# Moving two attention buffers by 128 bytes and several operands further into their places, in a one-core FoX/MLA decoder kernel

## The chip, the cores and the metric

The kernel runs on one core of one Trainium2 chip. The metric is device time in microseconds (us) of one launch. The kernel before takes 1050.32 us (median of 3 runs, 1049.77 to 1051.04). One further run was recorded by the hardware profiler; all rows of the profile come from that one.

## The reference, cut to what matters

One sequence of 256 tokens of width 1024 passes through two layers, in float32. A layer is a half feed-forward step, a mixer, a second half feed-forward step and a gated per-layer embedding, each followed by a layer norm. The mixer is a "forgetting" attention (FoX, 16 heads of 64) in layer 0 and a multi-head latent attention (MLA, 16 heads) in layer 1:

```python
x = post_norm(x, 0.5 * swiglu(x, w_in, w_out), ...)      # D_FF = 2816
x = post_norm(x, fox_mixer(...) if layer == 0 else mla_mixer(...), ...)
x = post_norm(x, 0.5 * swiglu(x, w_in2, w_out2), ...)
x = post_norm(x, sigmoid(x @ Wg + bg) * (p[i] @ Wp), ...)

def mla_mixer(x, w_dq, q_norm, w_uq, w_o, k_nope, k_rope, v, cos, sin):
    c_q = rms_norm(x @ w_dq, q_norm)                       # 384 latents per token
    q = jnp.einsum('bsc,chd->bshd', c_q, w_uq)             # 16 heads x (128 + 64)
    s = q_nope . k_nope + rope(q_rope) . k_rope            # causal, blocks of 128 queries
    o = softmax(s * 192 ** -0.5) . v
    return o.reshape(B, S, 16 * 128) @ w_o
```

The keys and values of the MLA layer come from 256 latents per token and one rotated key of 64 that all heads share (`shared_kv`).

## The kernel before, in words

**Numbers in two halves.** TensorE multiplies in the fp32r type. To keep float32 accuracy each operand is held as a rounded half ("hi") and a rest ("lo"), and each product is three matmuls that add into one PSUM bank: hi by hi, hi by lo, lo by hi (`mm3`, whose matmuls are all recorded under L616). A weight arrives by DMA as a 1 MB group in a raw buffer (`raw`); ScalarE writes hi (L252, L260), VectorE subtracts and writes lo (L253, L264). The pair goes to one of ten slots, which the profile calls `hl`. Activations are split in the same way out of PSUM: `high` (L629, ScalarE) and then `low` (L633, VectorE), which reads hi and so runs behind it.

**Two operands of a matmul.** One operand is loaded into the array and stays (a PEld row); the other streams past it (the PE row). The loading of the next one overlaps the streaming of the present one. Which of the two a weight is depends on the step: in the bulk of the first feed-forward product the weights (`wiu`) are loaded and the transposed stream `xT` moves; in its first columns (`win`) and in many other products (`fv`, `kvv`, `qr`, `pg`, `wout`, `fo`, `mo`) the weights move past a loaded activation.

**Where a buffer lies.** Pools place the tiles one behind another in each partition of on-chip memory, so that a tile's size sets the byte positions of all behind it. `place` (L221) puts a split weight into its slot of 2112 words; `moves` (L427) named the weights that start 48 words (192 bytes) into it: `fv` and `pg 0`. The rest start at word 0. Four buffers, `fs`, `qk`, `ota` and `otb` ("homes"), hold the hidden activations in the feed-forward steps and something else in the mixers. In the MLA layer `qk` holds the queries and keys of two heads, `ota` and `otb` the transposed attention outputs, `gb` the transposed query latents (`cqt`), and a part of `fs` the rotated keys (`kr`). With the sizes of before the slots, `fs`, `qk`, `gb` and `P` begin at 224 modulo 256 bytes, `xT` at 160, and `ota` and `otb` at 96.

**The order of work in the MLA layer.** A list written out by hand, `ORDER` (L71), names 527 steps; each emits its instructions at once, so the list sets the order on every engine. The steps of one head h: `gen` computes query and key in a PSUM bank, `ga` and `gd` write them into `qk` (ScalarE hi, VectorE lo), `QK` multiplies them (six matmuls of `tr<-qk` and three of `tr<-fs,xT`, which is the rotated part), `mi` adds the mask and takes minima (VectorE, L1717 and L1720), `ex` is the exponential (ScalarE, L1730), `T`, `ta` and `td` transpose the weights of attention into `PT`, `AV` multiplies with the values, `oa` and `od` write the result to `ota` or `otb`, and `O h` multiplies it with the output weights (`y<-hl,otb` and `y<-hl,ota`). Steps `f`, `l` and `a` split further weights meanwhile. `qk` holds heads of even and odd number apart: the index `s = h % 2` in `gen` and `h % 2` in `QK`. The list runs ahead: head h+1's `gen`, `ga` and `gd` often stand before `QK h`, for instance

```python
"f 1", "gen 6", "ga 6", "T 4", "ta 4", "td 4", "gd 6",
"tr 4", "a", "QK 5", "a", "a", "a", "mi 5", ...
```

**What sets the waits.** No wait is written by hand. The framework notes which part of which tile an instruction reads or writes, and where two instructions of different engines touch the same part it puts a semaphore wait on the later one. How finely parts are told apart follows from the shape in which the tile was made and how it is sliced.

Of the kernel before, what the change touches and what calls it, by code (L numbers as in the profile page):

```python
# [11 lines left out]
F32R = mybir.dt.float32r  # L12
# [132 lines left out]
class Stream:  # L145
# [74 lines left out]

    def place(self, key, slot):  # L221
        w = self.pool.tile([128, 2112], F32R, tag=slot, name=slot, bufs=1)
        c = 48 if moves(key) else 0
        return w[:, c : c + 2048].rearrange("p (i c) -> p i c", i=2)

    def split(self, half=False):
        self.later()
        nc = self.nc
        key = self.order[self.ready]
        g = group_of(key)  # L230
        while self.sums_left(key):
            self.add(g)
        src, parts, n = unit_of(key, self.raw[g], self.sums.get(g))
        if self.aside(key):
            w = self.pool.tile([128, 2, 512], F32R, tag="g4", name="g4", bufs=6)
        else:
            slot = self.slots.pop(0)
            self.slot_of[key] = slot
            w = self.place(key, slot)
        hi, lo = w[:parts, 0, :n], w[:parts, 1, :n]  # L240
        shape = src.shape
        if len(shape) == 3:
            hi = hi.rearrange("p (a b) -> p a b", b=shape[2])
            lo = lo.rearrange("p (a b) -> p a b", b=shape[2])
        elif len(shape) == 4:
            hi = hi.rearrange("p (a b c) -> p a b c", b=shape[2], c=shape[3])
            lo = lo.rearrange("p (a b c) -> p a b c", b=shape[2], c=shape[3])
        t = self.arrives[group_of(key)]
        self.act_t, self.dve_t = max(self.act_t, t), max(self.dve_t, t)

        def both():
            nc.scalar.activation(hi, src, AF.Copy)  # L252
            nc.vector.tensor_tensor(lo, src, hi.bitcast(F32), op=ALU.subtract)  # L253

        if key[0] == "pb":
            nc.gpsimd.memset(w[:, 0, :].bitcast(F32), 0.0)
            lo = w[32:33, 0, :n]
            both()
        elif half:
            nc.scalar.activation(hi, src, AF.Copy)  # L260
            self.busy(act=n)

            def rest():
                nc.vector.tensor_tensor(lo, src, hi.bitcast(F32), op=ALU.subtract)  # L264
                self.busy(dve=n)
                self.split_done(key, w)

            self.rest = rest
            return
        else:  # L270
            both()
        self.pair(n)
        self.split_done(key, w)

    def aside(self, key):
# [148 lines left out]
    return key  # L424


def moves(key):  # L427
    return key[0] == "fv" or key[:2] == ("pg", 0)


def unit_of(key, raw, sums=None):

    k, u = key[0], key[-1] % 2
    if k in ("win", "fv"):
        return raw.rearrange("p (k c) -> p k c", c=512)[:, 2 * u : 2 * u + 2, :], 128, 1024
    if k == "wiu":
        return raw[:, 1024 * u : 1024 * u + 1024], 128, 1024
    if k == "ws":
        i = key[-1]
        return ((raw, sums)[i // 2])[:, 1024 * u : 1024 * u + (512 if i == 3 else 1024)], 128, 512 if i == 3 else 1024  # L440
    if k == "fvc":
        n = 816 if key[-1] < 2 else 544
        return raw[:, n * u : n * u + n], 128, n
    if k in ("wout", "fvb", "fo", "pg", "pp", "mo", "qr"):
        return raw[:, 1024 * u : 1024 * u + 1024], 128, 1024
    if k in ("fk", "fq"):
        return raw.rearrange("p (k c) -> p k c", c=256)[:, :, 128 * u : 128 * u + 128], 128, 1024
    if k == "pb":
        return raw[0:1, 0:1024], 1, 1024
    if k == "kd":  # L450
        return raw[:, 640 * u : 640 * u + 640], 128, 640
    if k == "dq":
        return raw[:, 768 * u : 768 * u + 768], 128, 768
    if k == "qn":
        return raw[:, 512:1280], 128, 768
    if k == "kvv":
        return raw[:, 0:1024], 128, 1024
    if k == "kvk":
        return raw[:, 0:512], 128, 512
    raise KeyError(key)  # L460
# [50 lines left out]
class Trunk:  # L511
# [612 lines left out]
    def fox(self, li):  # L1124
        nc, S, a = self.nc, self.S, self.a
# [26 lines left out]
        def VC(t, at={}):  # L1152

            ps = self.bank("y")
            for k in range(8):
                if k in at:
                    at[k]()
                if k % 3 == 0:
                    w = self.use(("fvc", k // 3))
                c = 272 * (k % 3)  # L1160
                self.mm3(
                    ps[:, 0:272], lambda i: self.xT[:, t, i, k, :], lambda i: w[:, i, c : c + 272], k == 0, k == 7)
            if (t, 1) not in v:
# [1 line left out]
            o = v[t, 1]  # L1165
# [28 lines left out]
        f, e, u, r, ab = (fs[fr, 256 * i : 256 * i + 256] for i in range(5))  # L1194
# [79 lines left out]
        qk = self.own([128, 2, 2, 512], F32R, "qk")  # L1274
# [200 lines left out]

    def kv_transpose_rope(self):
        nc = self.nc
        self.kr = self.kvt[:, 1088:1856].rearrange("p (i t c) -> p t i c", t=2, i=3)
        kr = [self.kr[:, :, i, :] for i in range(3)]
        b = self.bank("tr")  # L1480
        for t in range(2):
# [20 lines left out]
    def mla(self, li):  # L1502
# [3 lines left out]
            self.dma(qn, pbcast(a["mla_q_norm"][0], QR))  # L1506
        scale = float(192 ** -0.5)
        v = {}
        cqt = self.tl([128, 2, 2, 3, 128], F32R, "gb", 1)
        cqtok = self.tl([128, 2, 768], F32, "PT", 1)  # L1510
        S.reclaim("otb", "qk")
        home = {}
# [163 lines left out]

        def gen(h):
            if h == 0:
                o = self.own([128, 2, 1072], F32R, "qk")
                home["qk"] = o[:, :, 0:1024].rearrange("p w (t i s c) -> p w t i s c", t=2, i=2, s=2)  # L1680
            ps = self.bank("h")
            hp, s = h // 2, h % 2
# [252 lines left out]
```

## Time and profile before

| | |
|---|---|
| median of 3 runs | 1050.32 us (1049.77 to 1051.04) |
| time of the profiled execution | 1049.6 us |
| its span (first to last instruction) | 1047.8 us |
| TensorE matmul (PE) | 1035.6 us busy, 99% of the span, 7085 matmuls |
| TensorE weight load (PEld) | 948.6 us, 91%, beside PE |
| VectorE (DVE) | 891.8 us, 85% |
| ScalarE (ACT) | 592.9 us, 57% |
| GpSimd (POOL) | 58.0 us, 6% |
| data moved | 202.74 MB, mean 193 GB/s |
| mean granted TensorE clock | 0.998 |

The profiled execution's own time is 1.8 us above its span, which is what lies around the first and the last instruction. A row of the timeline gives the start and the length in us of a run of like instructions, the engine, the line, the operation, `out<-in` by the program's buffer names, the shape, and how many it joins. In the length of a row of joined matmuls the pipelined end of the last is contained, so that the time of one matmul is better read as the start of the next row less the start of this one, over the count.

### The profile page before, as it was taken

How to read it: one execution, taken by the hardware profiler on the slowest of the kernel's cores; microseconds unless marked ns; L12 is line 12 of the kernel's file. 1: busy time of each engine (PE TensorE's matmuls, PEld its weight loads, DVE VectorE, ACT ScalarE, POOL GpSimd, SP SyncE). 2: the span in 40 equal slices, each digit the busy share in tenths (PEclk: the TensorE clock that was granted, in tenths of full speed). 3: DMA queues.
4: the chain of work that ended last, by engine and by line, in shares of the span. 5: the costliest groups of instructions: out<-in, count | busy, mean ns of one | idle time of the engine just before them, and what ended most of it. 6: DMA issues, size and time to landing. Idle time of an engine off the chain costs nothing.

```text
span 1047.8 us, 17555 instructions
## 1 busy us (share of the span) xinstructions
PE 1035.6 (99%) x7085; PEld 948.6 (91%) x7085; DVE 891.8 (85%) x1312; ACT 592.9 (57%) x901; POOL 58.0 (6%) x88
## 2 busy tenths in 40 slices
PE   9999999999999999999999999999999999999996
PEld 8999898899889999998899898988999889898986
DVE  5788977868898979978979899888887989889877
ACT  6555563666755555663565646646776564646541
POOL 0000000122300000000220000000000000000000
PEclk9999999999999999999999999999999999999999
DMA  7855586455636363673674545743445564555732
GB/s 281 305 191 188 185 298 243 162 168 169 216 128 246 121 252 125 241 282 132 236 260 151 195 169 190 270 142 112 145 156 179 183 214 162 200 190 176 271 125 81
DMA packets 37476, 202.74 MB, mean 193 GB/s; under 512 B 3970, under 2 KB 9874, under 8 KB 16532
## 3 DMA queue, kind: packets, MB, share of 16 engines
q1 hardware_dynamic: 37396, 201.63, 54.3%
q8 instruction: 55, 0.90, 0.3%
q14 instruction: 25, 0.20, 0.1%
HBM read 200.55 MB, written 1.06 MB: 192 GB/s over the span
## 4 chain that ended last, share of the span: by engine, by line
PE 95%; DVE 2%; ACT 1%; issue 1%; DMA 0%; SPq 0%; DVEq 0%; ACTq 0%
PE h L616 53%; PE y L616 29%; PE tr L616 10%; PE tr L620 2%; DVE hl L253 1%; PE h L620 1%; DMA raw<-in_w_dram 0%; PE tr L1375 0%; DVE ts L300 0%; DVE x L705 0%; DVE tr L1720 0%; ACT qk L629 0%; DVE PT L633 0%; DVE ts L306 0%; DVE raw L308 0%
## 5 line engine op out<-in xcount | busy, mean ns | idle before, releaser
L616 PE MATMUL h<-xT,hl 128*128 128x256 f32 x3144 | 366.1, 277 | 1.2 <-ACT hl L327 0.7
L616 PEld LDWEIGHTS h<-xT,hl 128*128 128x128 f32 x3144 | 362.0, 188 | 2.9 <-ACT hl L327 1.2
L253 DVE TENSOR_TENSOR hl<-raw,hl 128x1024 fp32r<-128x1024 f32 (+5 forms) x271 | 314.2, 1190 | 36.1 <-ACT hl L252 35.0
L252 ACT ACTIVATE hl<-raw 128x1024 fp32r<-128x1024 f32 (+5 forms) x271 | 267.8, 1027 | 70.6 <-DVE raw L308 41.3
L616 PE MATMUL y<-hl,g 128*128 128x512 f32 x336 | 78.6, 391 | 0.0
L616 PEld LDWEIGHTS y<-hl,g 128*128 128x128 f32 x336 | 62.5, 188 | 12.6
L616 PE MATMUL h<-hl,xT 128*128 128x512 f32 (+2 forms) x312 | 67.9, 371 | 0.0
L616 PEld LDWEIGHTS h<-hl,xT 128*128 128x128 f32 x312 | 54.9, 188 | 9.8
L616 PE MATMUL y<-hl,otb 128*128 128x512 f32 x219 | 58.0, 399 | 0.0
L264 DVE TENSOR_TENSOR hl<-raw,hl 128x1024 fp32r<-128x1024 f32 (+2 forms) x44 | 52.3, 1192 | 0.8 <-ACT hl L260 0.7
L616 PE MATMUL y<-hl,xT 128*128 128x512 f32 (+3 forms) x282 | 52.7, 334 | 0.0
L260 ACT ACTIVATE hl<-raw 128x1024 fp32r<-128x1024 f32 (+2 forms) x44 | 45.2, 1029 | 9.7 <-DVE raw L308 9.1
L629 ACT ACTIVATE xT<-tr 128x512 fp32r<-128x512 f32 x28 | 16.1, 597 | 58.9 <-PE tr L620 58.9
L616 PEld LDWEIGHTS y<-hl,xT 128*128 128x128 f32 x282 | 44.1, 188 | 4.6 <-ACT xT L629 0.4
L616 PEld LDWEIGHTS y<-hl,otb 128*128 128x128 f32 x219 | 39.8, 188 | 8.4 <-DVE otb L633 0.3
L616 PE MATMUL y<-hl,ota 128*128 128x512 f32 x177 | 46.8, 398 | 0.1
L700 POOL TENSOR_TENSOR rs<-ve,mhalf 128x1 f32<-128x1 f32 x16 | 15.1, 942 | 519.8 <-DVE ve L699 519.8
L616 PE MATMUL tr<-xT,hl 128*128 128x256 f32 x360 | 42.5, 277 | 0.0
L616 PEld LDWEIGHTS tr<-xT,hl 128*128 128x128 f32 x360 | 41.7, 188 | 0.4
L616 PEld LDWEIGHTS y<-hl,ota 128*128 128x128 f32 x177 | 32.7, 189 | 7.7 <-DVE hl L253 0.6
L823 ACT ACTIVATE P<-h 128x512 f32<-128x512 f32 x33 | 19.7, 596 | 33.0 <-PE h L616 32.6
L300 DVE TENSOR_TENSOR ts<-raw 128x1024 f32<-128x1024 f32 x29 | 35.4, 1222 | 0.6
(322 smaller groups left out, 1632.7 us busy)
## 6 DMA issues: line engine op xcount, KB each, us to landing
raw<-in_ffn_in_dram SPq DMA_DIRECT2D x85, 1024.0 KB, 5.0
raw<-in_ffn_out_dram SPq DMA_DIRECT2D x44, 1024.0 KB, 5.0
raw<-in_pg_dram SPq DMA_DIRECT2D x8, 1024.0 KB, 4.9
raw<-in_mo_dram SPq DMA_DIRECT2D x8, 1024.0 KB, 4.8
raw<-in_kq_dram SPq DMA_DIRECT2D x8, 640.0 KB, 4.2
gb<-in_ln_g_dram SPq DMA_DIRECT2D x8, 512.0 KB, 5.9
gb<-in_ln_b_dram SPq DMA_DIRECT2D x8, 512.0 KB, 7.5
raw<-in_fk_dram SPq DMA_DIRECT2D x4, 1024.0 KB, 5.6
```

Of the source, the lines that this page charges most:

```text
L252: nc.scalar.activation(hi, src, AF.Copy)
L253: nc.vector.tensor_tensor(lo, src, hi.bitcast(F32), op=ALU.subtract)
L260: nc.scalar.activation(hi, src, AF.Copy)
L264: nc.vector.tensor_tensor(lo, src, hi.bitcast(F32), op=ALU.subtract)
L300: tt(s[:, 0:1024].rearrange("p (a b) -> p a b", b=512), r[:, 0:512][:, None, :].to_broadcast([128, 2, 512]), r[:, 512:1536].rearrange("p ( ...
L616: self.nc.tensor.matmul(out, lhsT, rhs, start=start, stop=stop)
L620: self.nc.tensor.transpose(out, in_, self.ident)
L629: self.nc.scalar.activation(hi, src, AF.Copy)
L700: nc.gpsimd.tensor_tensor(rs, ve, self.mhalf, op=ALU.pow)
L823: nc.scalar.activation(gt, ps, AF.Silu)
```

## The change

Two kinds of edits. The first is in `place` and in the sizes of tiles. A table `shift` takes the place of `moves`: the weights `win` (but for the first feed-forward step of layer 0), `kvv` and `qr` start 48 words into their slots too, as `fv` and `pg 0` did; `fvb` and `fvc` start 32 words in, `kd` 36 and `dq` 40. The three column blocks of `fvc` lie 320 words apart in place of 272. The rotated keys start at word 1120 of their buffer in place of 1088 (128 bytes), and the query latents 48 words into `gb`. The second is in `gen`: the `qk` tile is made as one flat row of 2176 words, whose first 2144 are then viewed as two parts of 1072, where it was made as [128, 2, 1072]. It is 32 words (128 bytes) longer, so that `ota` and `otb`, and what lies behind them, lie 128 bytes further on. `ota` and `otb` then begin at 224 modulo 256.

```diff
--- before.py
+++ after.py
@@ -220,7 +220,7 @@
 
     def place(self, key, slot):
         w = self.pool.tile([128, 2112], F32R, tag=slot, name=slot, bufs=1)
-        c = 48 if moves(key) else 0
+        c = shift(key)
         return w[:, c : c + 2048].rearrange("p (i c) -> p i c", i=2)
 
     def split(self, half=False):
@@ -240,8 +240,9 @@
         hi, lo = w[:parts, 0, :n], w[:parts, 1, :n]
         shape = src.shape
         if len(shape) == 3:
-            hi = hi.rearrange("p (a b) -> p a b", b=shape[2])
-            lo = lo.rearrange("p (a b) -> p a b", b=shape[2])
+            b = n // shape[1]
+            hi = hi.rearrange("p (a b) -> p a b", b=b)[:, :, 0 : shape[2]]
+            lo = lo.rearrange("p (a b) -> p a b", b=b)[:, :, 0 : shape[2]]
         elif len(shape) == 4:
             hi = hi.rearrange("p (a b c) -> p a b c", b=shape[2], c=shape[3])
             lo = lo.rearrange("p (a b c) -> p a b c", b=shape[2], c=shape[3])
@@ -269,7 +270,7 @@
             return
         else:
             both()
-        self.pair(n)
+        self.pair(math.prod(shape[1:]))
         self.split_done(key, w)
 
     def aside(self, key):
@@ -424,8 +425,11 @@
     return key
 
 
-def moves(key):
-    return key[0] == "fv" or key[:2] == ("pg", 0)
+def shift(key):
+
+    if key[0] in ("fv", "kvv", "qr") or key[:2] == ("pg", 0) or key[0] == "win" and key[1:3] != (0, "ffn1"):
+        return 48
+    return {"fvb": 32, "fvc": 32, "kd": 36, "dq": 40}.get(key[0], 0)
 
 
 def unit_of(key, raw, sums=None):
@@ -440,7 +444,7 @@
         return ((raw, sums)[i // 2])[:, 1024 * u : 1024 * u + (512 if i == 3 else 1024)], 128, 512 if i == 3 else 1024
     if k == "fvc":
         n = 816 if key[-1] < 2 else 544
-        return raw[:, n * u : n * u + n], 128, n
+        return raw[:, n * u : n * u + n].rearrange("p (a b) -> p a b", b=272), 128, n // 272 * 320
     if k in ("wout", "fvb", "fo", "pg", "pp", "mo", "qr"):
         return raw[:, 1024 * u : 1024 * u + 1024], 128, 1024
     if k in ("fk", "fq"):
@@ -1157,7 +1161,7 @@
                     at[k]()
                 if k % 3 == 0:
                     w = self.use(("fvc", k // 3))
-                c = 272 * (k % 3)
+                c = 320 * (k % 3)
                 self.mm3(
                     ps[:, 0:272], lambda i: self.xT[:, t, i, k, :], lambda i: w[:, i, c : c + 272], k == 0, k == 7)
             if (t, 1) not in v:
@@ -1475,7 +1479,7 @@
 
     def kv_transpose_rope(self):
         nc = self.nc
-        self.kr = self.kvt[:, 1088:1856].rearrange("p (i t c) -> p t i c", t=2, i=3)
+        self.kr = self.kvt[:, 1120:1888].rearrange("p (i t c) -> p t i c", t=2, i=3)
         kr = [self.kr[:, :, i, :] for i in range(3)]
         b = self.bank("tr")
         for t in range(2):
@@ -1506,7 +1510,7 @@
             self.dma(qn, pbcast(a["mla_q_norm"][0], QR))
         scale = float(192 ** -0.5)
         v = {}
-        cqt = self.tl([128, 2, 2, 3, 128], F32R, "gb", 1)
+        cqt = self.tl([128, 1584], F32R, "gb", 1)[:, 48:1584].rearrange("p (t i k c) -> p t i k c", t=2, i=2, k=3)
         cqtok = self.tl([128, 2, 768], F32, "PT", 1)
         S.reclaim("otb", "qk")
         home = {}
@@ -1676,7 +1680,7 @@
 
         def gen(h):
             if h == 0:
-                o = self.own([128, 2, 1072], F32R, "qk")
+                o = self.own([128, 2176], F32R, "qk")[:, 0:2144].rearrange("p (w c) -> p w c", w=2)
                 home["qk"] = o[:, :, 0:1024].rearrange("p w (t i s c) -> p w t i s c", t=2, i=2, s=2)
             ps = self.bank("h")
             hp, s = h // 2, h % 2
```

No instruction is added, removed or reordered on any engine, as far as the names go. The waits differ. The lines of the changed kernel's matmuls are numbered L620 (L616 before) and its transposes L624 (L620 before).

First place: TensorE around `QK 2` in the MLA layer. The rows `tr_7712<-qk` are that step, `tr_7704<-ident,P` the transpose before it, `h_7747<-PT` the attention output after it. Before:

```order
L616 MATMUL h_7697<-p_7667,g_7358 128x128 [waits Activation_49]
L620 MATMUL tr_7704<-ident,P 128x128 x3
L616 MATMUL tr_7712<-qk 128x256 [waits PE_49]
L616 MATMUL tr_7712<-qk 128x128
L616 MATMUL tr_7712<-fs,xT 128x256
L616 MATMUL tr_7712<-qk 128x256 x3
L616 MATMUL tr_7712<-fs,xT 128x256 x2
L616 MATMUL h_7747<-PT,g_7383 128x256 [waits DVE_49,Activation_49]
L616 MATMUL h_7747<-PT,g_7383 128x256 [waits DVE_49]
```

and in the changed kernel:

```order
L620 MATMUL h_7697<-p_7667,g_7358 128x128 [waits Activation_49]
L624 MATMUL tr_7704<-ident,P 128x128 x3
L620 MATMUL tr_7712<-qk 128x256 [waits DVE_49]
L620 MATMUL tr_7712<-qk 128x128
L620 MATMUL tr_7712<-fs,xT 128x256
L620 MATMUL tr_7712<-qk 128x256 x3
L620 MATMUL tr_7712<-fs,xT 128x256 x2
L620 MATMUL h_7747<-PT,g_7383 128x256 [waits Activation_49]
L620 MATMUL h_7747<-PT,g_7383 128x256 [waits DVE_49]
```

The first matmul of `QK 2` waited on a TensorE count and now waits on a VectorE count, and the first matmul behind the step has lost its VectorE wait.

Second place: TensorE around `QK 5`, where `h_7923` (rows with `fs,hl` and `gb,hl`) is `gen 6`, `tr_7953<-qk` is `QK 5`, and `y_7732<-hl_7788,otb` is the output product that follows. Before:

```order
L616 MATMUL h_7923<-gb,hl_7846 128x256 x9
L620 MATMUL tr_7940<-ident,P 128x128 [waits PE_49,Activation_49]
L620 MATMUL tr_7940<-ident,P 128x128 [waits Activation_49]
L620 MATMUL tr_7940<-ident,P 128x128
L616 MATMUL tr_7953<-qk 128x256 [waits DVE_49]
L616 MATMUL tr_7953<-qk 128x128
L616 MATMUL tr_7953<-fs,xT 128x256
L616 MATMUL tr_7953<-qk 128x256 x3
L616 MATMUL tr_7953<-fs,xT 128x256 x2
L616 MATMUL y_7732<-hl_7788,otb 128x512 [waits Activation_49]
L616 MATMUL y_7732<-hl_7788,otb 128x512
L616 MATMUL y_7732<-hl_7788,otb 128x512 [waits DVE_49]
```

and in the changed kernel:

```order
L620 MATMUL h_7923<-gb,hl_7846 128x256 x9
L624 MATMUL tr_7940<-ident,P 128x128 [waits PE_49,Activation_49]
L624 MATMUL tr_7940<-ident,P 128x128 [waits Activation_49]
L624 MATMUL tr_7940<-ident,P 128x128
L620 MATMUL tr_7953<-qk 128x256 [waits DVE_49,Activation_49]
L620 MATMUL tr_7953<-qk 128x128
L620 MATMUL tr_7953<-fs,xT 128x256
L620 MATMUL tr_7953<-qk 128x256 x3
L620 MATMUL tr_7953<-fs,xT 128x256 x2
L620 MATMUL y_7732<-hl_7788,otb 128x512 x3
L620 MATMUL y_7733<-hl_7788,otb 128x512 x3
```

The first matmul of `QK 5` waited on VectorE alone and now waits on VectorE and ScalarE. The ScalarE and the VectorE wait of the output product behind it are gone, since `QK 5` has waited for more by then.

Third place: VectorE at `gd 11`, the write of lo of head 11 (`qk<-h_8347`), which stands behind `QK 10` in the list. `otb<-h_8329` is the attention output's lo, `tr_8372` the scores of `QK 10`. Before:

```order
L633 TENSOR_TENSOR otb<-h_8329,otb 128x256 [waits Activation_49]
L253 TENSOR_TENSOR hl_8342<-raw,hl_8342 128x768 [waits Activation_49]
L633 TENSOR_TENSOR qk<-h_8347,qk 128x2x2x128 [waits Activation_49]
L633 TENSOR_TENSOR PT<-tr_8364,PT 128x2x128 [waits PE_49,Activation_49]
L1717 TENSOR_TENSOR P<-tr_8372,mask 128x128 [waits PE_49]
L1720 ISA tr_8372,nm<-tr_8372,P 128x128 [waits DVE_49]
```

and in the changed kernel:

```order
L637 TENSOR_TENSOR otb<-h_8329,otb 128x256 [waits Activation_49]
L254 TENSOR_TENSOR hl_8342<-raw,hl_8342 128x768 [waits Activation_49]
L637 TENSOR_TENSOR qk<-h_8347,qk 128x2x2x128 [waits PE_49]
L637 TENSOR_TENSOR PT<-tr_8364,PT 128x2x128 [waits Activation_49]
L1721 TENSOR_TENSOR P<-tr_8372,mask 128x128 [waits PE_49]
L1724 ISA tr_8372,nm<-tr_8372,P 128x128 [waits DVE_49]
```

The write waited on ScalarE alone, and now on TensorE.

## The prediction

> **What bounds the kernel now.** I read the page's first lines, the chain of waits, and the stretch with the MLA attention from the busy times by stretch.
>
> ```profile
> span 1047.8 us, 17555 instructions
> PE 1035.6 (99%) x7085; PEld 948.6 (91%) x7085; DVE 891.8 (85%) x1312; ACT 592.9 (57%) x901; POOL 58.0 (6%) x88
> PE 95%; DVE 2%; ACT 1%; issue 1%; DMA 0%; SPq 0%; DVEq 0%; ACTq 0%
> 730.00:810.00 80.00, 79.47 (x544) 72.53 (x543) 67.82 (x169) 57.48 (x145) 0.00 (x0) 1.00 0.44 149
> ```
>
> TensorE matmul sets the time: 95% of the chain, and in the stretch from 730 to 810 us it is busy for 79.47 of 80, with VectorE at 67.82 and ScalarE at 57.48. So two things move the end: how fast matmuls follow each other, and any wait that stops TensorE. The change touches both.
>
> **Part 1, the places: matmuls follow each other faster.** Matmuls of one shape don't all take the same time here. In one feed-forward product of layer 0 the stationary operand comes from `qk`, then `ota`, then `otb`; shape and source of the weights are the same.
>
> ```profile
> 413.79 1.52 PE L616 MATMUL y<-hl,qk 128*128 128x512 f32 x6
> ...
> 418.55 1.56 PE L616 MATMUL y<-hl,ota 128*128 128x512 f32 x6
> ...
> 423.43 1.56 PE L616 MATMUL y<-gb,otb 128*128 128x512 f32 x6
> ...
> 428.31 0.87 PE L616 MATMUL h<-xT,hl 128*128 128x256 f32 x6
> ```
>
> From 413.79 to 418.55 stand 21 matmuls, 226.7 ns each; from 418.55 to 423.43 and from there to 428.31 also 21 each, 232.4 ns. What differs is where the operands lie: the moving `hl` begins at 224 modulo 256 bytes, `qk` (the next to be loaded) at 224, `ota` and `otb` at 96. Distance 0 gives 226.7, distance 128 gives 232.4. The other distances:
>
> ```profile
> 848.12 6.58 PE L616 MATMUL h<-hl,xT 128*128 128x512 f32 x28
> 854.54 0.63 PE L616 MATMUL tr<-xT,hl 128*128 128x256 f32 x4
> ...
> 195.48 2.99 PE L616 MATMUL h<-hl,xT 128*128 128x256 f32 x24
> 198.31 0.41 PE L616 MATMUL y<-hl,xT 128*128 128x272 f32 x2
> ...
> 406.29 2.88 PE L616 MATMUL h<-xT,hl 128*128 128x256 f32 x24
> 409.01 1.54 PE L616 MATMUL y<-hl,fs 128*128 128x512 f32 x6
> ...
> 749.71 1.23 PE L616 MATMUL h<-gb,hl 128*128 128x256 f32 x9
> 750.78 0.49 PE L620 MATMUL tr<-ident,P 128*128 128x128 f32 x3
> ```
>
> Weights (224) past `xT` (160), distance 64: 6.42 us for 28, 229.3 ns. With 256 columns, distance 64 (`fvb`): 2.83 for 24, 117.9 ns, against 2.72 for 24, 113.3 ns, where `xT` moves past `hl`. Latents in `gb` (distance 0, in two stretches): 1.07 for 9, 118.9 ns.
>
> I counted the program's matmuls by distance in both versions. 547 with 512 columns go from 128 to 0 (most of them `y<-hl,otb` and `y<-hl,ota`); 290 go from 64 to 0 (`win`, `kvv`, `qr` and others), 34 from 192 to 0, 142 of the latents from 0 to 192. At full price: 547 x 5.7 ns = 3.1 us; 290 x 2.6 = 0.75; 34 x 5 (no row at 192; I set it near 128's) = 0.2; 142 x 5.6 = 0.8. I take five sixths of each, 4.05, since most stand in groups of six among other shapes and the border of a group may keep its price. Distances that no row shows: 64 `fvb` matmuls at 192 (0 to 0.3 us, by 117.9 against 113.3) and 130 of `kd`, `dq`, `fvc` with 272 to 384 columns (0 to 0.5, 5.7 ns scaled by columns): half of each, 0.4. The rotated keys move few matmuls. `xT` past `ota` and `otb` (288 with 256 columns) goes from 64 to 192, where `xT` past `hl` is already, and the two cost the same before:
>
> ```profile
> L616 PE MATMUL h<-xT,hl 128*128 128x256 f32 x3144 | 366.1, 277 | 1.2 <-ACT hl L327 0.7 <-DVE hl L329 0.4
> L616 PE MATMUL h<-xT,otb 128*128 128x256 f32 x192 | 23.1, 276 | 0.0
> ```
>
> Sum: **4.4 us gained**, with ends of 2.2 (547 and 290 at 2.6 ns, the rest nothing) and 5.7 (everything full). All of it lies on TensorE, so it counts in full while TensorE is the bound.
>
> The Trainium skill speaks against this part: in "TensorE: Matmul & The Clock Gate", section "Step-by-step: what each phase is for", it says that TensorE has two independent read ports, and that "Loading the next tile's weights doesn't steal SBUF read bandwidth from the running matmul." By that, where the operands lie would not matter and this part's term would be 0; the 226.7 against 232.4 ns disagree.
>
> **Part 2, the flat `qk` tile: nine new waits.** Made as [128, 2, 1072], the tile let the framework tell even from odd heads. Made as one row of 2176, it no longer does: in the order of the changed kernel `QK h` waits for the latest write of either head. Where `ga` and `gd` of head h+1 stand before `QK h` in the list, TensorE now waits for a write that it doesn't read. What that costs is read from the trace of before: the start of `QK h` against the end of that write. Nine are late (in order `QK` 2, 4, 5, 6, 8, 10, 11, 13, 14):
>
> ```profile
> 731.57 0.42 PE L616 MATMUL tr<-qk 128*128 128x256 f32 x2
> 731.58 0.68 DVE L633 TENSOR_TENSOR qk<-h,qk 128x512 fp32r<-128x512 f32 x1
> ...
> 744.78 0.95 DVE L253 TENSOR_TENSOR hl<-raw,hl 128x768 fp32r<-128x768 f32 x1
> ...
> 745.65 0.68 DVE L633 TENSOR_TENSOR qk<-h,qk 128x512 fp32r<-128x512 f32 x1
> ...
> 746.11 0.34 PE L616 MATMUL tr<-qk 128*128 128x256 f32 x2
> ...
> 751.03 0.43 PE L616 MATMUL tr<-qk 128*128 128x256 f32 x2
> ...
> 752.23 0.68 DVE L633 TENSOR_TENSOR qk<-h,qk 128x512 fp32r<-128x512 f32 x1
> ...
> 752.83 0.28 DVE L1717 TENSOR_TENSOR P<-tr,mask 128x128 f32<-128x128 f32 x1
> ...
> 757.78 0.95 DVE L264 TENSOR_TENSOR hl<-raw,hl 128x768 fp32r<-128x768 f32 x1
> ...
> 758.65 0.68 DVE L633 TENSOR_TENSOR qk<-h,qk 128x512 fp32r<-128x512 f32 x1
> ...
> 758.81 0.43 PE L616 MATMUL tr<-qk 128*128 128x256 f32 x2
> ...
> 779.61 0.43 PE L616 MATMUL tr<-qk 128*128 128x256 f32 x2
> ...
> 780.87 0.68 DVE L633 TENSOR_TENSOR qk<-h,qk 128x512 fp32r<-128x512 f32 x1
> ...
> 785.04 0.61 ACT L629 ACTIVATE qk<-h 128x512 fp32r<-128x512 f32 x1
> ...
> 785.07 0.43 PE L616 MATMUL tr<-qk 128*128 128x256 f32 x2
> ...
> 791.45 0.43 PE L616 MATMUL tr<-qk 128*128 128x256 f32 x2
> ...
> 792.03 0.69 DVE L633 TENSOR_TENSOR qk<-h,qk 128x512 fp32r<-128x512 f32 x1 [1.55 <-ACT qk L629]
> ...
> 801.54 0.35 PE L616 MATMUL tr<-qk 128*128 128x256 f32 x2
> ...
> 802.28 0.58 ACT L629 ACTIVATE qk<-h 128x512 fp32r<-128x512 f32 x1
> ...
> 806.58 0.45 PE L616 MATMUL tr<-qk 128*128 128x256 f32 x2
> ...
> 806.75 0.60 ACT L629 ACTIVATE qk<-h 128x512 fp32r<-128x512 f32 x1
> ```
>
> `QK 5` starts at 751.03; VectorE's write for head 6 ends at 752.23 + 0.68 = 752.91, so TensorE would stand for 1.88 us. In the same way `QK 2` 0.69, `QK 4` 0.22, `QK 6` 0.52, `QK 8` 1.94, `QK 11` 1.27; and by ScalarE's write of hi (that of lo comes behind `QK` in the list there) `QK 10` 0.58, `QK 13` 1.32, `QK 14` 0.77. Together 9.2 us.
>
> Do they add up? If TensorE is late by 0.69 at `QK 2`, and the other engines don't move with it, the next write is early by as much, and only the largest, 1.94, would be paid: that is the lower end. If they move with it, each is paid. Behind `QK h` in VectorE's queue stands its minima (L1717, at 752.83, hard on the end of the write), which needs the scores of `QK h`; and everything of head h+1 is queued behind that. The writes themselves need `gen` of head h+1, a TensorE product. So they move. `QK 4` and `QK 6` I leave out: their writes stand behind a weight split (744.78, 757.78), which TensorE doesn't feed, and the lateness of `QK 2` and `QK 5` (0.69, 1.88) is more than they ask. **8.5 us lost**, ends 1.9 and 9.2. What is late next is the minima, the exponential and the splits behind them; VectorE has 12 of 80 us in this stretch to catch up.
>
> Waits that fall away behind `QK` (ScalarE's and VectorE's on the output product) are worth nothing: the longer wait ahead contains them.
>
> **The sum.** -4.4 + 8.5 = +4.1 us. The profiled execution took 1049.6, so 1053.7; the median of the runs stands 0.7 above that execution, so **1054.4 us**. Own ends: 6 to 9.2 of waits less 5.7 to 2.2, so 1050.6 to 1057.3.
>
> **The rivals.**
> *B, faster: the waits mostly overlap each other.* Place: VectorE's and ScalarE's queues between the writes. If they run on while TensorE stands, one excess pays for all: 1.9 - 4.4 = -2.5, 1047.8 us. It decides from the point at which less than half of the 8.5 is paid. For it: ScalarE and VectorE do have splits that TensorE doesn't feed. Against: 752.83, above.
> *B', no change: about half of the waits is paid*, 4.2 - 4.4, 1050.1 us. For it: the splits before three of nine writes.
> *C, slower still: the places give nothing* (the waits alone), +8.5, 1058.8 us. Against: rows of one product with 226.7 and 232.4; for it: the distance is my reading of them, and 276 and 277 ns at two different distances don't show it. By the skill's rule above it would be this one.
> *D, the change to the tile makes no TensorE wait that bites* (the wait named in the order is on an earlier write), -4.4, 1045.9. Against: at `QK 2` a wait on VectorE takes the place of one on TensorE, where only head 3's write is new.
>
> **How the numbers follow.** The forecast 0.76, B 0.06, B' 0.08, C 0.06, D 0.04. Under 0.2% (2.1 us: 1048.2 to 1052.4) this kernel's measurement can't tell a change from none. B and D are faster: 0.10. B' and the forecast's lower edge (0.06) are the same: 0.14. The rest, 0.70, and C are slower: 0.76. The range 1050.1 to 1057.4 reaches to B' and holds the forecast's ends; it leaves out B, D and C, 0.16.
>
> **What would show it.** Part 1: in the changed kernel `y<-hl,ota` and `y<-hl,otb` at 226.7 ns like `qk`; 229.3 ns of `h<-hl,xT` likewise 226.7; the latents' 118.9 at 113.3. By 730 us, ahead of the first new wait, the changed kernel would be some 2.6 us earlier (313 of the 547, 181 of the 290, all of the 34, 35 of the 142, most of the rest). Part 2: idle time of TensorE ahead of `tr<-qk`, put down to VectorE or ScalarE with the tile `qk`, some 8 us in all; TensorE's busy share of that stretch near 90%. Wrong would be the forecast if that idle time is below 4 us (B, B'), or if the 232.4 stays (C).

## The result, and the profile after

The changed kernel takes 1055.95 us (median of 6 runs, 1054.48 to 1059.96) against 1050.47 us (6 runs) before: a ratio of 1.0059, 95% interval 1.0041 to 1.0077, or 6.2 us slower (4.3 to 8.1). The ratio, here and below, is formed from all the runs and not from the two medians, which lie 5.5 us apart. The forecast was 4.1 us slower.

The profiled execution took 1056.92 us. First three lines of the changed kernel's page: its span, the busy times and the chain. Then, from the busy times by stretch, the stretch of the MLA layer that the prediction reads.

```profile
span 1055.1 us, 17555 instructions
PE 1036.1 (98%) x7085; PEld 950.3 (90%) x7085; DVE 892.2 (85%) x1312; ACT 594.3 (56%) x901; POOL 60.2 (6%) x88
PE 90%; DVE 6%; ACT 2%; issue 1%; DMA 0%; DVEq 0%; SPq 0%; ACTq 0%
```

```profile
730.00:810.00 80.00, 73.54 (x476) 65.69 (x475) 59.40 (x146) 51.56 (x126) 0.00 (x0) 0.96 0.41 139
```

TensorE's busy time is what it was, but the chain now runs through VectorE for 6% (2% before) and ScalarE for 2% (1%). In the MLA stretch TensorE is busy for 73.54 of 80 us, where it was 79.47. The column behind the five engines is the granted clock: 0.96 there, 1.00 before.

The waits of TensorE in the changed kernel (engine, tile and line of the waiting instruction, the releaser; us in all, times, longest):

```profile
PE tr L620 <- DVE qk L637: 5.2, 4, 1.8
PE tr L620 <- ACT qk L633: 2.3, 3, 1.2
PE y L596 <- POOL mhalf L581: 1.2, 1, 1.2
PE h L620 <- ACT p L633: 0.4, 1, 0.4
```

The first two rows are new: `QK` waits for writes of `qk`, seven times, 7.5 us. The same view of the kernel before has no row with `tr` and `qk`. The idle time in such a row begins at the modelled end of the last matmul; by the later start of `QK` against before the seven cost more, 9.0 us (the table below).

The places, in the same stretches as before. First the feed-forward product with `qk`, `ota` and `otb` loaded, then the latents, then the weights past `xT` (the timeline's TensorE rows):

```profile
411.36 1.52 PE L620 MATMUL y<-hl,qk 128*128 128x512 f32 x6
...
416.12 1.52 PE L620 MATMUL y<-hl,ota 128*128 128x512 f32 x6
...
420.88 1.52 PE L620 MATMUL y<-gb,otb 128*128 128x512 f32 x6
...
425.64 0.63 PE L620 MATMUL h<-xT,hl 128*128 128x256 f32 x4
...
756.54 1.18 PE L620 MATMUL h<-gb,hl 128*128 128x256 f32 x9
757.56 0.52 PE L620 MATMUL h<-PT,g 128*128 128x256 f32 x3
...
856.41 6.51 PE L620 MATMUL h<-hl,xT 128*128 128x512 f32 x28
862.75 0.87 PE L620 MATMUL tr<-xT,hl 128*128 128x256 f32 x6
```

All three homes now take 4.76 us for 21 matmuls, 226.7 ns; before, `ota` and `otb` took 232.4. The weights past `xT` take 6.34 us for 28, 226.4 ns (229.3 before), the latents 1.02 for 9, 113.3 ns (118.9 before). Both parts of the change show in the trace as the prediction had them.

Where the 7.3 us of span went, by the start of each of the 7085 matmuls against the same one before: the first 10 us are 0.9 earlier (TensorE waited less for its first split weights in this execution, 0.2 us against 0.7 and 0.4); from there to 730 us 2.3 more are gained; the late heads lose 9.1 in steps; two groups of slow matmuls behind the stalls of `QK 5` and `QK 9` lose 3.1; what else is left from 730 us on is a gain of 1.7. That makes +7.3.

| | step forecast | step seen |
|---|---|---|
| QK 2 | 0.69 | 0.76 |
| QK 4 | 0.22 (left out) | 0.06 |
| QK 5 | 1.88 | 2.03 |
| QK 6 | 0.52 (left out) | under 0.1 |
| QK 9 ("QK 8" in the prediction) | 1.94 | 2.09 |
| QK 10 | 0.58 | 0.60 |
| QK 11 | 1.27 | 1.33 |
| QK 13 | 1.32 | 1.37 |
| QK 14 | 0.77 | 0.83 |

The slow matmuls were not foreseen. They stand in the changed kernel behind `QK 5`, first in the timeline and then in the busy times of these 10 us:

```profile
750.48 0.42 PE L620 MATMUL tr<-qk 128*128 128x256 f32 x2 [1.78 <-DVE qk L637]
...
751.50 2.33 PE L620 MATMUL y<-hl,otb 128*128 128x512 f32 x6
753.63 2.37 PE L620 MATMUL tr<-hl,fs 128*128 128x512 f32 x6
755.84 0.85 PE L620 MATMUL h<-fs,hl 128*128 128x256 f32 x6
```

```profile
750.00:760.00 10.00, 9.52 (x51) 8.29 (x52) 6.47 (x15) 6.99 (x15) 0.00 (x0) 0.83 0.32 86
```

Twelve matmuls take 4.34 us, 362 ns each, where 227 to 232 is the rule, and the granted clock in these 10 us is 0.83 on average: 0.50 for 3.41 us, from 752.00 on, and 1.00 in the rest. Experiment 7 comes back to it.

### The profile page after: what moved, and what is told of

It reads as the page before. It is cut to its first block, busy times and chain, and to the rows that moved or that the text cites. A ratio compares the mean times of both kernels' runs of the same rounds, so it can differ in the third digit from the quotient of the medians.

```text
span 1055.1 us, 17555 instructions
## 1 busy us (share of the span) xinstructions
PE 1036.1 (98%) x7085; PEld 950.3 (90%) x7085; DVE 892.2 (85%) x1312; ACT 594.3 (56%) x901; POOL 60.2 (6%) x88
## 4 chain that ended last, share of the span: by engine, by line
PE 90%; DVE 6%; ACT 2%; issue 1%; DMA 0%; DVEq 0%; SPq 0%; ACTq 0%
PE h L620 50%; PE y L620 27%; PE tr L620 10%; PE tr L624 2%; DVE hl L254 2%; DVE ts L301 1%; ACT qk L633 1%; PE h L624 1%; ACT hl L253 0%; DVE ts L307 0%; DVE raw L309 0%; DVE tr L1724 0%; DVE qk L637 0%; DVE PT L637 0%; DVE g L254 0%
## 5 line engine op out<-in xcount | busy, mean ns | idle before, releaser
L620 PE MATMUL h<-xT,hl 128*128 128x256 f32 x3144 | 365.8, 277 | 0.2 <-DVE hl L330 0.2
L620 PEld LDWEIGHTS h<-xT,hl 128*128 128x128 f32 x3144 | 362.2, 189 | 1.4 <-ACT xT L633 0.6
L620 PE MATMUL y<-hl,g 128*128 128x512 f32 x336 | 78.6, 391 | 0.0
L620 PEld LDWEIGHTS y<-hl,g 128*128 128x128 f32 x336 | 62.5, 188 | 12.6
L620 PE MATMUL h<-hl,xT 128*128 128x512 f32 (+2 forms) x312 | 67.7, 370 | 0.0
L620 PEld LDWEIGHTS h<-hl,xT 128*128 128x128 f32 x312 | 55.1, 188 | 9.4
L620 PE MATMUL y<-hl,otb 128*128 128x512 f32 x219 | 59.0, 405 | 0.0
L620 PE MATMUL y<-hl,xT 128*128 128x512 f32 (+3 forms) x282 | 52.3, 333 | 0.0
L620 PEld LDWEIGHTS y<-hl,otb 128*128 128x128 f32 x219 | 40.8, 194 | 8.1 <-DVE otb L637 0.3
L620 PEld LDWEIGHTS y<-hl,xT 128*128 128x128 f32 x282 | 43.7, 188 | 4.6 <-ACT xT L633 0.3
L620 PE MATMUL y<-hl,ota 128*128 128x512 f32 x177 | 46.0, 394 | 0.2 <-DVE hl L254 0.2
L620 PE MATMUL tr<-xT,hl 128*128 128x256 f32 x360 | 42.6, 277 | 0.0
L620 PEld LDWEIGHTS tr<-xT,hl 128*128 128x128 f32 x360 | 41.8, 188 | 0.4
L620 PEld LDWEIGHTS y<-hl,ota 128*128 128x128 f32 x177 | 32.6, 188 | 7.1 <-DVE hl L254 0.6
```

Of the source, the lines that this page charges most:

```text
L620: self.nc.tensor.matmul(out, lhsT, rhs, start=start, stop=stop)
```

## The experiments

The ratios are to runs of the kernel before on the same chips, whose median was 1049.4 to 1050.6 us there; 0.1% is 1.05 us.

**1. The places alone.** The positions of the changed kernel without its waits.

```diff
-                o = self.own([128, 2176], F32R, "qk")[:, 0:2144].rearrange("p (w c) -> p w c", w=2)
+                o = self.own([128, 2, 1072], F32R, "qk")
-        return tag, self.own([128, 2, 896], F32R, tag)
+        return tag, self.own([128, 2, 1088 if tag == "qk" else 896], F32R, tag)[:, :, 0:896]
```

> All positions of the changed kernel, byte for byte, but the qk tile of the mixer is again [128, 2, 1072] (the 32 words are added by making the feed-forward home of the same place [128, 2, 1088]); the order and the waits are then those of the kernel before. Theory (two effects that add up): no idle time of TensorE ahead of tr<-qk, y<-hl,ota and y<-hl,otb at 226.7 ns a matmul, and by the spacing of matmuls in the changed kernel 3.4 us are gained: about 1047.1 against 1050.5. Rival (the places give nothing, or shifting buffers costs elsewhere): 1050.5 or more.

Measured: 1047.01 us, ratio 0.9966 (0.9955 to 0.9977), 3.6 us faster than before and, by the two ratios, 9.8 faster than the changed kernel. Its page's span (the profiled execution is the fastest of the nine), and from the view of waits the two longest of TensorE:

```profile
span 1042.4 us, 17555 instructions
```

```profile
PE y L596 <- POOL mhalf L581: 1.2, 1, 1.2
PE h L620 <- ACT p L633: 0.4, 1, 0.4
```

No `tr` waits for `qk`. The intended part of the change works, and this kernel beats both.

By classes, from the time between the starts of neighbouring matmuls here and before (start-up stretches and matmuls that waited left out): the 547 give 2.4 us, the 290 give 0.47, the latents 0.43, those from 192 to 0 0.17, `fvb` 0.14; the `kd` weights lose 0.30.

**2. The waits, with a move of 32 bytes.**

```diff
-                o = self.own([128, 2, 1072], F32R, "qk")
+                o = self.own([128, 2152], F32R, "qk")[:, 0:2144].rearrange("p (w c) -> p w c", w=2)
```

(against the kernel before)

> The kernel before with the changed kernel's waits and none of its shifted operands: qk is made as one row of 2152 words whose first 2144 are viewed as two parts, so that ota and otb move by 32 bytes (distance 96 in place of 128, which 14 matmuls of the trace before show at the same 232.4 ns). Theory: the nine stalls in full, 9.1 us by the steps seen in the changed kernel, and 3.1 us of matmuls at a lower granted clock behind the two stalls of 2 us: about +12, 1062.6. Rival (the clock drop belongs to the changed kernel's other positions): +9, 1059.5. Rival (stalls overlap): +2 to +5.

Measured: 1064.43 us, ratio 1.0133 (1.0120 to 1.0146), 14 us slower, more than either theory. The stalls are there (5.3 and 2.5 us in the view of waits), but in the profiled execution the granted clock stayed at 1.00 behind them, so slow matmuls are not the reason for the excess. The next run is. The edit also does a little more than was meant: in the built program the waits of TensorE are those of the changed kernel, but 17 instructions of ScalarE and VectorE, most of them writes of `qk`, wait otherwise than there.

**3. The 32 bytes without the waits.** A tile that is never used lengthens the place of `qk`.

```diff
+                self.tl([128, 2152], F32R, "qk", 1)
                 o = self.own([128, 2, 1072], F32R, "qk")
```

> The kernel before with everything behind qk 32 bytes further on, as in the run with the waits and a 32-byte move, but with the order and the waits of before. Theory (the 4 to 5 us that the other run lost beyond the nine stalls come from the 32 bytes): 1054 to 1055. Rival (32 bytes cost 1.4 us, by the matmuls whose distance changes there, and the waits cost the rest): 1052.

Measured: 1053.57 us, ratio 1.0038 (1.0026 to 1.0050): 4.0 us slower for 32 bytes, as the theory has it (4 to 5 us). So the waits in experiment 2 cost 1.0133 less 1.0038, 0.95%, 10.0 us.

**4. The homes alone, without and with the waits.** Both are the kernel before with `ota` and `otb` 128 bytes further on; the first by the longer feed-forward home as in experiment 1, the second by the changed kernel's `qk` tile.

> The kernel before with ota and otb 128 bytes further on (through a longer feed-forward home) and nothing else: no shifted weights, latents or keys, order and waits as before. Theory (distance decides): the matmuls of 512 columns that went from 128 to 0 give their 2.4 us and those from 192 to 0 0.2 us; 1048.0 against 1050.6, and y<-hl,ota at 226.7 ns while weights past xT stay at 229.3 ns. Rival (all positions behind qk matter, or none): same time as the run with the places alone, 1047.0, or as before, 1050.6.

> The kernel before with the changed kernel's qk tile alone (one row of 2176 words, 2144 of them viewed as two parts), so with ota and otb 128 bytes further on and with the nine waits, but with no shifted weights, latents or keys. Theory (parts add up): 1050.6 - 2.6 + 9 = 1057.0. Rival (the run with the waits and a 32-byte move, 1064.4, shows what the waits cost, 13.8): 1061.8.

Measured: the homes alone 1047.18 us, ratio 0.9979 (0.9969 to 0.9989), 2.2 us faster; with the waits 1056.52 us, ratio 1.0070 (1.0058 to 1.0082), 7.4 slower. The difference, 0.91%, is 9.6 us for the waits. Both runs come out near the theory (2.6 us faster and 6.4 slower) and away from the rivals. The product with `ota` and `otb` loaded, in the run of the homes alone:

```profile
418.61 1.52 PE L616 MATMUL y<-hl,ota 128*128 128x512 f32 x6
...
423.37 1.52 PE L616 MATMUL y<-gb,otb 128*128 128x512 f32 x6
```

From the one row to the other are 21 matmuls in 4.76 us, 226.7 ns, as in the changed kernel, though no weight was moved.

Three pairs with the same positions thus give the price of the waits: 9.8 us (changed kernel, 1.0059, less the places alone, 0.9966), 9.6 and 10.0. Each is uncertain by about 2 us (an estimate from the intervals of its two ratios). In the profiles of the same three pairs the steps at the nine late heads make 9.0, 9.0 and 9.3 us. Within that uncertainty the price is the same in all three, so waits and places add up.

**5. The next head's writes behind QK.** The changed kernel, with its tile and its positions; for each of the nine late heads `ga` and `gd` of the next head move (ahead of `QK` 10, 13 and 14 `ga` alone, as `gd` stood behind already), for instance

```diff
-    "f 1", "gen 6", "ga 6", "T 4", "ta 4", "td 4", "gd 6", "tr 4", "a", "QK 5", "a",
+    "f 1", "gen 6", "T 4", "ta 4", "td 4", "tr 4", "a", "QK 5", "ga 6", "gd 6", "a",
```

> The changed kernel with its positions and its qk tile, but at the nine late heads (QK 2, 4, 5, 6, 9, 10, 11, 13, 14) the steps ga and gd of the next head that stood ahead of QK now stand directly behind it. Theory (the nine waits are the whole loss): QK finds nothing to wait for; TensorE idles less than 1 us in all ahead of tr<-qk, and the kernel comes near the run with the places alone, 1047 to 1048.5. Rival (the later writes only move the stall, to the next product of that head): 1051 to 1056, with idle time ahead of other TensorE rows.

Measured: 1050.20 us, ratio 1.0009 (1.0000 to 1.0018). Between the two: the order takes away 5 of the 9.8 us and loses the rest elsewhere, as the waits of TensorE show:

```profile
PE h L617 <- DVE qk L634: 1.0, 2, 0.8
PE h L617 <- DVE PT L634: 0.8, 2, 0.6
PE h L617 <- ACT p L630: 0.4, 1, 0.4
PE tr L617 <- ACT g L1548: 0.4, 1, 0.4
```

The product of the attention weights and others (`h`, `tr`) now wait behind the later writes. By the starts of the matmuls this profile loses 3.6 us between 730 and 810 us of the kernel before, where that of the places alone gains 0.4. So with this order the stalls move on. Whether another order would hide them wholly was not tried.

**6. Filling the wait.**

```diff
             b = self.bank("tr")
+            for _ in range({5: 2, 9: 2}.get(h, 0)):
+                self.nc.tensor.matmul(b[:, 0:384], self.mask[:, 0:128], self.mask, start=True, stop=True)
```

> The changed kernel with two matmuls of the mask (384 columns, float32, about 0.65 us each, into the bank that QK clears) ahead of QK 5 and of QK 9, so that TensorE idles there for some 0.5 us in place of 1.8. The writes that QK waits for are not touched. Theory (the idle time itself lowers the granted clock): the stalls end at the same time, the matmuls behind them keep 227 to 232 ns in place of 430, and the kernel is 3.1 us faster than the changed one, about 1053. Rival (the lower clock has another cause, such as the transfers or the order of work there): no gain, 1056, clock low at the same two places.

Measured: 1056.94 us, ratio 1.0058 (1.0045 to 1.0071): no gain. In its profile the filled stall of `QK 5` leaves 0.49 us idle, and the matmuls behind the stalls keep their time (here the six behind `QK 9`; then the busy times of the 10 us around `QK 5`, with the clock at 1.00):

```profile
750.65 1.46 PE L1705 MATMUL tr<-mask 128*128 128x384 f32 x4
752.59 0.42 PE L620 MATMUL tr<-qk 128*128 128x256 f32 x2 [0.49 <-DVE qk L637]
...
784.15 1.56 PE L620 MATMUL y<-hl,otb 128*128 128x512 f32 x6
785.55 0.52 PE L620 MATMUL h<-PT,g 128*128 128x256 f32 x3
```

```profile
750.00:760.00 10.00, 9.51 (x58) 7.92 (x57) 7.26 (x17) 7.76 (x19) 0.00 (x0) 1.00 0.19 54
```

The rival was missed too: it had the clock low at these places. The clock was full, but the 3 us did not come off the median. By the starts of the matmuls this execution does gain them: it is 1.5 us earlier behind each of the two stalls than the changed kernel's first profile, 3.0 in all. But it had lost 2.2 us to that profile in the first 100 us, where the two kernels are the same, and the next experiment shows that the changed kernel itself loses the 3 us in some executions only.

**7. The changed kernel once more**, unchanged.

> The changed kernel itself once more. In its first profile the granted clock fell to 0.77 to 0.83 behind the stalls of QK 5 and QK 9, worth about 3 us; in the runs with the waits and a 32-byte move, and with the filling matmuls, the same stalls of 2.0 us left the clock at 1.00. Theory (the drop belongs to single executions and not to the kernel): without it the profile has the nine stalls, 9.2 us, and a span of 1051 to 1053; median 1055 to 1056.5. Rival (the drop belongs to this kernel's stalls, and the filling took it away): again 0.8 at the same two places, span 1054 to 1056.

Measured: 1055.58 us, ratio 1.0057 (1.0044 to 1.0070). In the profile the clock stays full behind `QK 5` and falls behind `QK 9`:

```profile
751.38 0.42 PE L620 MATMUL tr<-qk 128*128 128x256 f32 x2 [1.78 <-DVE qk L637]
...
752.41 1.54 PE L620 MATMUL y<-hl,otb 128*128 128x512 f32 x6
...
781.97 0.49 PE L620 MATMUL tr<-qk 128*128 128x256 f32 x2 [1.84 <-DVE qk L637]
...
783.65 2.44 PE L620 MATMUL y<-hl,otb 128*128 128x512 f32 x6
```

The six output matmuls take 1.54 us behind the one stall and 2.44 behind the other, though the idle times are alike (1.78 and 1.84). So neither expectation holds as it stands: the median is the theory's, the span of this execution (1054.6 us) the rival's. The drop goes with single executions, and within one with single stalls. Over the profiles of the changed kernel (two), of the homes with the waits and of experiment 2, the long stalls number eight, and four of them are followed by slow matmuls (in the kernel of experiment 4 behind `QK 5`, in that of experiment 2 behind neither). Behind the two filled stalls, and behind the shorter ones (up to 1.3 us idle), none is.

The kept traces show which four. The record of the granted clock changes only in steps of 3.41 us on one grid in each execution: in the changed kernel's first profile it is full for 744.11, then 27.31, then 262.83 us, which are 218, 8 and 77 such steps, and half (0.50) for one step after the first and one after the second. The four stalls that were followed by slow matmuls lie inside one step each, and end 0.18 us or more before its end; the next step is the one at half the clock. Of the other four, two run across the border of two steps (both in experiment 2) and two end within 0.06 us of it. So for these eight it is the stall's place on the grid, which differs from execution to execution, that goes with the drop. This is read from eight stalls; no run set the place on purpose.

The executions without a profile fit. Of the changed kernel's eleven, the five with a mean granted clock of 0.994 to 0.996 took 1056.36 to 1059.96 us, and the six with 0.997 to 0.999 took 1054.48 to 1055.58. (Of the five of the kernel with the homes and the waits, in experiment 4, the one above 0.996 took as long as the fastest others, 1056.5 us.) Over all kernels with the long stalls, 9 of 20 executions are at 0.996 or below; of the 122 executions of the other kernels, the filled one among them, none is.

**8. Other distances for ota and otb.** As experiment 3, with 2160 and 2192 words, so 64 and 192 bytes.

> The kernel before with everything behind qk 64 bytes further on (ota and otb at 160, distance 64 of the moving weights), order and waits as before. Theory (distance decides, by the value that other matmuls have at it): y<-hl,ota and y<-hl,otb at 229.3 ns, so 1.1 us gained in the 547 of 512 columns; xT past ota and otb goes to distance 0. Rival (it is the 128 bytes alone that count): 226.7 or 232.4.

> As the run before, with 192 bytes (ota and otb at 32, distance 192). Theory: y<-hl,ota and y<-hl,otb at 231.9 ns, as other matmuls at distance 192; no change of the time. Rival: the distance counts only up to 64 or 128 either way, 229.3 or 226.7.

Measured: 1053.05 us, ratio 1.0032 (1.0020 to 1.0044), and 1053.32 us, ratio 1.0037 (1.0024 to 1.0050). The price per matmul is as the theory has it; the times are not. The same product in the run with 64 bytes, then in the run with 192:

```profile
419.02 1.54 PE L616 MATMUL y<-hl,ota 128*128 128x512 f32 x6
...
423.83 1.53 PE L616 MATMUL y<-gb,otb 128*128 128x512 f32 x6
```

```profile
418.28 1.56 PE L616 MATMUL y<-hl,ota 128*128 128x512 f32 x6
...
423.18 1.56 PE L616 MATMUL y<-gb,otb 128*128 128x512 f32 x6
```

From `ota` to `otb` are 21 matmuls: 4.81 us, 229.0 ns at distance 64, and 4.90 us, 233.3 ns at 192. What the theory left out is in another group, `xT` moving past `ota` and `otb`. In the first run it goes from distance 64 to 0 and in the second to 128 (the group of the run with 64 bytes, then of that with 192):

```profile
L616 PE MATMUL h<-xT,otb 128*128 128x256 f32 x192 | 24.3, 283 | 0.0
```

```profile
L616 PE MATMUL h<-xT,otb 128*128 128x256 f32 x192 | 24.1, 281 | 0.0
```

Before they took 276 ns, so 5 to 7 ns more for each. Over all 288 of them 1.75 and 1.36 us are lost, by the spacing of their starts, and in the 32-byte run 0.86. At 64 bytes this takes back the 1.6 us that the matmuls with 512 columns gain. A further 1.8 to 2.4 us in each of these three runs lies in `h<-xT,hl` and its like, whose two operands did not move in relation to each other; their cause was not found. There it lies in a few stretches of 50 to 100 us, in which `h<-xT,hl` takes 118 ns a matmul in place of 113. The two kernels with 32 bytes (experiments 2 and 3) have two of these stretches in common, from 625 to 675 and from 950 to 1000 us of the kernel before. In the first 125 us, however, such stretches also stand in the profiles of the homes alone and of experiments 5, 9 and 10, so that one profile does not show that a move caused them.

**9. The raw buffers alone by 32 bytes.** A tile of 1544 words that is never used lengthens the place of `PT`.

> The kernel before with only the buffers behind PT 32 bytes further on, the raw weight buffers among them; ota, otb and PT itself stay. The 32-byte move of everything behind qk cost 4 us, of which matmuls whose own distance changed make up 1.5. Theory (raw lies badly there, in the way of something that runs beside the matmuls): +2.5, 1052.5. Rival (the rest comes from ota, otb or PT): no change, 1050.

Measured: 1050.64 us, ratio 1.0008 (0.9999 to 1.0017). The rival: 0.8 us (-0.1 to 1.8), so that the 2.5 us of the theory are excluded. The position of `raw` is at most a part of what costs the 4 us.

**10. The kd weights back in place.**

```diff
-    return {"fvb": 32, "fvc": 32, "kd": 36, "dq": 40}.get(key[0], 0)
+    return {"fvb": 32, "fvc": 32, "dq": 40}.get(key[0], 0)
```

(against experiment 1)

> As the run with the places alone, but the weights kd start at word 0 again as before. In the changed kernel the 48 matmuls of 320 columns take 153 ns in place of 147. Theory: these go back to 147, 0.3 us less than the run with the places alone, about 1046.8, a difference that the times can't show and the rows of the 320-column matmuls can. Rival (the 153 ns come from something else in that stretch): they stay at 153.

Measured: 1047.64 us, ratio 0.9968 (0.9957 to 0.9980), no difference in time from experiment 1. The groups of the 320-column matmuls in the kernel before, in the changed one and in this one:

```profile
L616 PE MATMUL h<-hl,xT 128*128 128x320 f32 x48 | 7.4, 308 | 0.0
```

```profile
L620 PE MATMUL h<-hl,xT 128*128 128x320 f32 x48 | 7.7, 316 | 0.0
```

```profile
L620 PE MATMUL h<-hl,xT 128*128 128x320 f32 x48 | 7.4, 308 | 0.0
```

Moving `kd` by 36 words makes its matmuls slower, 0.3 us in all, and moving it back undoes that.

## Why the prediction was right, point by point

- **What bounds the kernel.** Right: every gain and loss was on TensorE. VectorE and ScalarE did the same work in the same time.
- **The 547 matmuls.** 2.4 us by the classes and 2.2 by the run of the homes alone, for 2.6.
- **The other classes.** The 290 gave 0.47 for 0.63, the latents 0.43 for 0.66, `fvb` 0.14 for 0.15. For `kd`, `dq` and `fvc` the prediction put a range from nothing to a gain; `kd` was outside it, a loss of 0.3. The sum by the run was 3.6 us (2.4 to 4.7) for 4.4. The five sixths that were taken for the borders were still too many. By 730 us the changed kernel was to be 2.6 us earlier; it is 3.2, of which 0.9 come from the start-up, so 2.3 from the places.
- **The rule of the Trainium skill** ("TensorE: Matmul & The Clock Gate", section "Step-by-step: what each phase is for"), by which a load of weights takes no read bandwidth from the running matmul, would have the time of a matmul the same wherever the two operands lie. Here the measurement differs from that by 2.5%: with `ota` and `otb` alone moved, their matmuls went from 232.4 to 226.7 ns. Whether it is read bandwidth that they share, no run shows. Rival C is out.
- **The nine waits.** The mechanism, the places and the sizes were right: seven heads by 0.60 to 2.09 us for 0.58 to 1.94, each 0.02 to 0.15 more than the end of the write, and `QK 4` and `QK 6` covered. The steps make 9.1 us, the three pairs 9.6 to 10.0, for 8.5. By the steps this term was 0.6 us too small, and the missing hand-over behind the write explains that. By the pairs it was 1.1 to 1.5 too small, which their uncertainty of about 2 us does not set apart from the 0.6. A part of what lies beyond 9.1 is the slow matmuls, which the prediction doesn't have: the changed kernel's executions with the lower mean clock (median 1056.7 us) took 1.3 us more than the others (1055.4), and they are five of eleven.
- **Do they add up?** Yes. Rivals B and B', in which the stalls overlap, would have shown 1.9 to 4.2 us, and each of the seven stalls was paid in full. Against D, the trace has the idle time.
- **The name of a head.** The row at 779.61 us belongs to `QK 9`, not `QK 8`; the write is that of head 10. The number was read from the right row.
- **Why the waits are there.** The prediction put them down to the tile being one row. That was too wide: versions with one row of 2144 words viewed as two parts, and with one row of 2176 viewed as two parts of 1088, have the order and the waits of before, by their built orders (neither was run). The waits came with two parts that do not fill the row: 2 x 1072 of 2176, or of 2152.
- **The range.** It holds the measured time, but its ends take 6 to 9.2 us for the waits, and the 6 is worked out nowhere: the prediction's own lower end for them was 1.9.
- **The sum.** +4.1 forecast, +6.2 measured (4.3 to 8.1), so the forecast lies just under the interval. Of the 2.1 us between them 0.8 come from the places and, by the pairs, 1.1 to 1.5 from the waits. Both errors go the same way, so that none of the agreement is owed to errors that cancelled.

## What to carry to other kernels

Padding a tile to move what lies behind it can change which accesses the framework holds apart: compare the waits of the built order, not only the order of the instructions, and pad in a tile that is not sliced there. In this kernel the mend was worth more than the change: with the same positions and the old waits, 3.6 us faster than before in place of 6.2 slower. The price of a new wait could be read from the trace before to about 10%: the end of the new producer less the start of the waiting instruction, each counted in full where the producer's engine is itself fed by the waiting one.

## What the runs showed of the hardware that was not expected

- **Distance between operands.** The time of a matmul with 512 columns in one piece went with the position of its moving operand less that of the next loaded one, modulo 256 bytes: 226.7 ns at 0, 229.0 at 64, 232.4 at 128, 233.3 at 192. It is the difference and not one operand's own position: in the trace before, the median is 227 ns where both begin at 160 and where both begin at 224, and 231 to 233 at distance 128 for three different pairs of positions. With 256 columns as two pieces of 128 (`xT`, latents) 0 was the worst: the latents take 118.9 ns at 0 and 113.3 at 192, and `xT` past `ota` and `otb` 113 at 64 and 192, 120 at 0. For this shape the distance is not all, as `h<-PT,g` takes 117 to 118 ns (median) at 192 before and at 64 in the changed kernel. The distance that was best for the one shape was worst for the other, so that a position suits both only if they are asked for different distances; the 128 bytes did that here (0 for the weights, 192 for `xT`), and 64 bytes did not. Why it is so was not tried.
- **Moves also counted where no distance changed.** The moves of 32, 64 and 192 bytes each cost 3.4 to 4.0 us, of which the matmuls with changed distances explain less than 2. And with the homes alone moved by 128 bytes, matmuls of the last stage whose two operands both stayed went faster; in the kernel before, and then with the homes moved:

```profile
1028.88 0.52 PE L616 MATMUL y<-qk,xT 128*128 128x256 f32 x3
1029.24 0.52 PE L616 MATMUL y<-fs,xT 128*128 128x256 f32 x3
```

```profile
1027.40 0.50 PE L616 MATMUL y<-qk,xT 128*128 128x256 f32 x3
1027.74 0.50 PE L616 MATMUL y<-fs,xT 128*128 128x256 f32 x3
```

Three take 0.36 us before and 0.34 then, 120 and 113 ns each by these rows. It is no accident of one execution: over this stage these matmuls take 113 ns in all eight profiles that have the homes 128 bytes on, and 117 to 119 in all six that have them elsewhere. In that stage VectorE reads `ota`, which did move. Whether the reads of other engines are the cause was not tried; it stays open.
- **A lower clock behind stalls.** After four of eight stalls of about 1.8 us idle the granted clock was half for one step of 3.41 us; up to twelve matmuls were slow, and some 1.5 us were lost. After stalls of up to 1.3 us it never fell. The four are those that lay inside one step of the clock's record with 0.18 us or more to spare at its end, so the same stall in the same kernel cost the 1.5 us in one execution and not in the next. Filling two stalls to some 0.5 us idle left the clock full in that profile, and no execution of that kernel has a mean clock below 0.997; its median is no lower for it, which its spread and a late start in the profiled execution leave open.
